# Two of the stores of a matmul-scale-add kernel are issued after a count of ScalarE's copies

## The chip, the cores and the metric

One core of one Trainium2 chip runs the whole program. The metric is the device time of one execution in microseconds (us); the median of three runs stands for a kernel. A profile is of one execution, with times counted from its first instruction.

## The reference

```python
def setup_inputs():
    batch, m, k, n = 16, 512, 1024, 768
    return {
        "x": np.random.randn(batch, m, k).astype(np.float32),
        "weight": np.random.randn(k, n).astype(np.float32),
        "scale": np.float32(0.1),
        "add_value": np.random.randn(batch, m, n).astype(np.float32),
    }

def reference(x, weight, scale, add_value):
    return (scale * np.matmul(x, weight) + add_value).astype(np.float32)
```

With the batch folded into the rows this is one product of 8192 x 1024 by 1024 x 768, scaled, plus a tensor of the result's size. In float32 x is 33.6 MB, add_value and the result are 25.2 MB each, and the weight is 3.1 MB: 87 MB in all.

## The kernel before

**Tiles.** The 8192 rows are 64 tiles of 128 rows. Each partition holds 16 consecutive rows of each block of 2048 (`R = 16`), so a transfer of 8 tiles is one long contiguous run for each partition. SBUF holds 16 tiles of x in float32 (`xs`, 16 slots) and 32 slots of `ao`, in which the tile's add_value lands, the result is made in place, and from which it is stored. The weight first lands in `ao` and is cast to bf16 into `w_bf`.

**The engines.** Every engine has its own hand-written stream, and they meet only at semaphores.

- SyncE issues every transfer in the order of the list `STREAM` (line 22): `w`, `x`, `a` are loads of weight, x and add_value, `o` is a store; the two numbers are the first tile and the count. `sync_engine` (line 87) walks the list. Before an issue it waits for what the transfer needs, through `need(sem, value)`, which emits a wait only if no earlier one on that semaphore was as high. All transfers go through one queue, in that order. The first load of x (line 225) and the last store (line 237) stand outside the list.
- ScalarE and GpSimd (`mover`, line 134) copy x from `xs` into `va`, cast to bf16. A move is four tiles; each of the two engines makes 8 copies for it, and each copy adds 1 to `by_act` or `by_pool`. There are 16 moves and so 128 copies on each engine. A move waits for its x to land (`x_sem`) and for a buffer of `va` to be free (`turned`).
- VectorE (`vector_engine`, line 150) transposes a half move (two tiles) at a time into `xt` (line 162), and finishes two tiles at a time: `ao = mm * scale + ao` from PSUM (line 171), which adds 2 to `made`.
- TensorE (line 205) multiplies: 8 weight loads and 16 matmuls a tile, in PSUM buffers for four tiles.

**Waits on SyncE.** A load of x waits until both copying engines have passed the move that was in its slots (lines 104 and 105). An add_value load waits for the one before it, and from tile 32 on for the landing of the store that frees its slots (lines 109 to 115). A store waits for the store two before it (line 125) and for its own tiles to be made (line 126). Around the change the order of issues is

```python
("x", 32, 8), ("o", 0, 8), ("o", 8, 8), ("a", 32, 8), ("x", 40, 8),
("a", 40, 8), ("x", 48, 8), ("o", 16, 8), ("o", 24, 8), ("a", 48, 4), ("x", 56, 4),
```

Of the kernel before, what the change touches and what calls it, by code (L numbers as in the profile page):

```python
# [27 lines left out]
]  # L28
FIRST, LAST = (0, 8), (56, 8)


@with_exitstack
def kernel(
# [26 lines left out]
    def rows(view, s, n):  # L60
        assert s // R == (s + n - 1) // R
        return view[:, s // R, s % R:s % R + n, :]
# [15 lines left out]
    by_act, by_pool, pool_go, turned, casts, done, made = (  # L78
        tc.alloc_semaphore(name)
        for name in ("by_act", "by_pool", "pool_go", "turned", "casts", "done", "made"))  # L80
# [3 lines left out]
    def slot(t):  # L84
        return (t + G) % A_SLOTS

    def sync_engine(eng):
        loads, stores, known = [], [], {}

        def need(sem, value):  # L90
            if known.get(sem, 0) < value:
                eng.wait_ge(sem, value)
                known[sem] = value

        for op, s, n in STREAM:
            last = s + n - 1
            if op == "w":
                dst = ao[:, s:s + n, :].rearrange("p (c r) n -> p c (r n)", r=2)
                move, sem = eng.dma_start(dst, w_v[:, s // 2:(s + n) // 2, :]), w_sem[s // 4]
            elif op == "x":  # L100
                k = s % X_SLOTS
                if last >= X_SLOTS:
                    moved = 8 * (last + 1 - X_SLOTS) // MOVE
                    need(by_act, moved)
                    need(by_pool, moved)
                move = eng.dma_start(xs[:, k:k + n, :], rows(x_v, s, n))
                sem = x_sem[k // MOVE]
            elif op == "a":
                if loads and s % G == 0:
                    need(a_sem, 16 * len(loads))  # L110
                if slot(s) == 0:
                    need(casts, KJ)
                if s >= A_SLOTS:
                    i = next(j for j, (a, b) in enumerate(stores) if a <= s - A_SLOTS < a + b)
                    need(o_sem[i % 2], 16 * (i // 2 + 1))
                move = eng.dma_start(ao[:, slot(s):slot(s) + n, :], rows(add_v, s, n))
                if s % G:
                    sem = a_late
                else:
                    sem = a_sem  # L120
                    loads.append((s, n))
            else:
                i = len(stores)
                if i > 1:
                    need(o_sem[i % 2], 16 * (i // 2))
                need(made, MADE + last + 1)
                move = eng.dma_start(rows(out_v, s, n), ao[:, slot(s):slot(s) + n, :])
                sem = o_sem[i % 2]
                stores.append((s, n))
            move.then_inc(sem, 16)  # L130
            if op == "x" and n == 2 * MOVE:
                eng.sem_inc(x_sem[k // MOVE + 1], 16)
# [90 lines left out]
    s, n = FIRST  # L223
# [4 lines left out]
    with tc.tile_critical(no_gpsimd_drain=True):  # L228
        sync_engine(nc.sync)
        mover(nc.scalar, nc.scalar.copy, 0, by_act)  # L230
        nc.scalar.addr_align(HALF_BLOCK, offset=PAST)
        mover(nc.gpsimd, nc.gpsimd.tensor_copy, 1, by_pool, pool_go)
        nc.gpsimd.addr_align(HALF_BLOCK, offset=PAST)
        vector_engine(nc.vector)
        tensor_engine(nc.tensor)
    s, n = LAST
# [36 lines left out]
```

## Time and profile before

| | us |
|---|---|
| median of 3 runs (209.06 to 209.6) | 209.28 |
| span of the profiled execution | 207.5 |
| TensorE busy | 168.4 |
| VectorE busy | 97.8 |
| ScalarE busy | 134.7 |
| GpSimd busy | 135.4 |

The span runs from the first to the last instruction of the program; the time of a run also holds what lies around it, which the profile of this execution doesn't give by itself. In the profile an engine's name with a q (SPq) is its sequencer, which issues transfers. "DMA" in a slice is the mean busy share of the core's 16 DMA engines. The time to landing of a transfer counts from its issue until all 16 engines have reported, so it holds the time in the queue. Line numbers are those of the kernel before.

### The profile page before, as it was taken

What the parts mean: (1) busy time and instruction counts of PE and PEld (TensorE: products, weight loads), DVE (VectorE), ACT (ScalarE), POOL (GpSimd) and SP (SyncE); (2) the same over time, 40 slices, a digit from 0 to 9 for tenths busy, and PEclk for the clock granted to TensorE, in tenths of its full rate; (3) what the DMA queues carried; (4) which work ended last, traced back from release to release, by engine and by line L of the source; (5) the groups of instructions that cost most, each with busy time, mean ns of one, the idle gap of its engine ahead of it and who ended that gap; (6) DMA issues with size and microseconds to landing.
All of it is one profiled execution on the core that took longest, in us unless ns stands there. A gap on an engine that the chain in (4) does not pass through costs nothing.

```text
span 207.5 us, 2310 instructions
## 1 busy us (share of the span) xinstructions
PE 168.4 (81%) x1024; PEld 50.3 (24%) x512; DVE 97.8 (47%) x66; ACT 134.7 (65%) x129; POOL 135.4 (65%) x132
## 2 busy tenths in 40 slices
PE   0000099999999999999999999999999999999400
PEld 0000023333332222222233333333333333333100
DVE  0005525537555555555555554755555555553300
ACT  2059970799999796969696079999970999300000
POOL 0049994799999996969696079999990899400000
PEclk9999999999999999999999999999999999999955
DMA  7999999999999999999999999999999999999993
GB/s 291 417 381 469 403 466 404 455 455 404 404 467 442 411 398 486 393 441 407 445 436 423 423 436 455 411 445 412 441 414 422 437 445 455 460 417 388 412 441 171
DMA packets 4147, 87.06 MB, mean 420 GB/s; under 512 B 432, under 2 KB 432, under 8 KB 944
## 3 DMA queue, kind: packets, MB, share of 16 engines
q1 hardware_dynamic: 4144, 87.03, 98.1%
q14 instruction: 3, 0.02, 0.0%
HBM read 61.87 MB, written 25.17 MB: 419 GB/s over the span
## 4 chain that ended last, share of the span: by engine, by line
PE 81%; DMA 6%; ACT 5%; DVE 1%; issue 1%; DVEq 0%; ACTq 0%
PE mm L197 81%; DMA xs<-in_x_dram 6%; ACT va L147 5%; DVE ao L171 1%; DVE xt L162 1%; ACTq L140 0%; DVEq L160 0%; DVEq L168 0%
## 5 line engine op out<-in xcount | busy, mean ns | idle before, releaser
L197 PE MATMUL mm<-w_bf,xt 128*128 128x512 bf16 (+1 forms) x1024 | 168.4, 328 | 26.0 <-DVE xt L162 26.0
L147 POOL CAST va<-xs 32x1024 bf16<-32x1024 f32 x128 | 135.2, 1056 | 43.1 <-DMA xs<-in_x_dram 24.7
L147 ACT CAST va<-xs 32x1024 bf16<-32x1024 f32 x128 | 133.4, 1042 | 42.1 <-DMA xs<-in_x_dram 25.8
L171 DVE SCALAR_TENSOR_TENSOR ao<-mm,ao 128x1536 f32 (+1 forms) x32 | 56.3, 1758 | 76.5 <-PE mm L197 76.5
L195 PEld LDWEIGHTS <-xt 128*128 128x128 bf16 x512 | 50.3, 98 | 143.6 <-issue 117.6
L162 DVE STREAM_TRANSPOSE xt<-va 128x1024 f32<-128x1024 f32 x32 | 39.4, 1234 | 3.8 <-ACT va L147 2.1
L155 DVE CAST w_bf<-ao 128x3072 bf16<-128x3072 f32 x2 | 4.5, 2240 | 18.1 <-DMA ao<-in_weight_dram 18.1
L136 ACT ACT_TABLE_LOAD x1 | 1.3, 1283 | 1.3 <-SPq L228 1.3
L254 POOL MEMSET const-float32-0.0<- 128x1 f32 x1 | 0.1, 98 | 0.2 <-issue 0.2
L254 POOL MEMSET const-bfloat16-1.0<- 128x1 bf16 x1 | 0.1, 100 | 0.0
L254 POOL MEMSET const-float32-1.0<- 128x1 f32 x1 | 0.1, 98 | 0.0
L254 POOL MEMSET const-uint8-127<- 128x1 uint8 x1 | 0.1, 97 | 0.0
## 6 DMA issues: line engine op xcount, KB each, us to landing
xs<-in_x_dram SPq DMA_DIRECT2D x7, 4096.0 KB, 20.9
ao<-in_add_value_dram SPq DMA_DIRECT2D x7, 3072.0 KB, 17.0
out_dram<-ao SPq DMA_DIRECT2D x6, 3072.0 KB, 27.0
out_dram<-ao SPq DMA_DIRECT2D x1, 6144.0 KB, 35.4
xs<-in_x_dram SPq DMA_DIRECT2D x2, 2048.0 KB, 19.1
ao<-in_weight_dram SPq DMA_DIRECT2D x2, 1536.0 KB, 16.8
ao<-in_add_value_dram SPq DMA_DIRECT2D x2, 1536.0 KB, 14.9
```

Of the source, the lines that this page charges most:

```text
L136: eng.preload_act_table(mybir.ActivationFunctionType.Copy)
L147: copy(va[q % VA_BUFS][32 * b:32 * b + 32, :, a, :], src[32 * a:32 * a + 32, :, b, :]).then_inc(count, 1)
L155: eng.tensor_copy(w_bf[:, s:s + n, :], ao[:, s:s + n, :]).then_inc(casts, n)
L162: eng.transpose(xt[:, 2 * half:2 * half + 2, :, :].rearrange("p i c m -> p (i c m)"), va[move % VA_BUFS][:, q:q + 2 * KC, :, :].bitcast(fp ...
L171: eng.scalar_tensor_tensor(a, mm[:, q:q + 2, 0:N], float(scale), a, op0=mybir.AluOpType.mult, op1=mybir.AluOpType.add).then_inc(made, 2)
L195: eng.ldweights(x_j, tile_position=(0, 0))
L197: m = eng.add_instruction(mybir.InstMatmult(start_tensor_calc=(j == 0), stop_tensor_calc=(j == KJ - 1), tile_size=(P, P), tile_position=(0 ...
L254: nc = _bacc.Bacc("TRN2", target_bir_lowering=False, num_devices=1)
```

## The change

Before the store that starts with tile 0, SyncE also waits until ScalarE has made 58 of its copies, and before the store that starts with tile 16 until it has made 93. No other line is touched.

```diff
 FIRST, LAST = (0, 8), (56, 8)
+HOLD = {0: 58, 16: 93}
...
                 if i > 1:
                     need(o_sem[i % 2], 16 * (i // 2))
                 need(made, MADE + last + 1)
+                if s in HOLD:
+                    need(by_act, HOLD[s])
                 move = eng.dma_start(rows(out_v, s, n), ao[:, slot(s):slot(s) + n, :])
                 sem = o_sem[i % 2]
                 stores.append((s, n))
```

## The prediction

> **What bounds the kernel now.** I read the page first, then the chain of waits, then the sync engine's queue in order of time, then single transfers.
>
> The page's busy times, the slices of PE, clock and DMA, the queue's share, and the start of the chain by line:
>
> ```profile
> PE 168.4 (81%) x1024; PEld 50.3 (24%) x512; DVE 97.8 (47%) x66; ACT 134.7 (65%) x129; POOL 135.4 (65%) x132
> ...
> PE   0000099999999999999999999999999999999400
> ...
> PEclk9999999999999999999999999999999999999955
> DMA  7999999999999999999999999999999999999993
> ...
> q1 hardware_dynamic: 4144, 87.03, 98.1%
> ...
> PE mm L197 81%; DMA xs<-in_x_dram 6%; ACT va L147 5%; DVE ao L171 1%; DVE xt L162 1%; ACTq L140 0%; DVEq L160 0%; DVEq L168 0%
> ```
>
> Two resources are full. TensorE has one unbroken stretch at full granted clock, and the 16 DMA engines are busy for 98.1% of the span. The chain names TensorE, because after its last matmul there is only one finish and one store:
>
> ```profile
> 26.01 168.37 PE mm L197 x1024
> ...
> 194.48 1.76 DVE ao L171
> ```
>
> The last finish ends at 196.24 us. What comes after it is read from the sync engine's queue (start, us, what it issued):
>
> ```profile
> 72.62 0.33 SPq L106 DMA_DIRECT2D xs<-in_x_dram  x1
> 73.05 0.85 SPq L127 DMA_DIRECT2D out_dram<-ao  x2
> 96.01 0.34 SPq L116 DMA_DIRECT2D ao<-in_add_value_dram  x1
> 96.44 0.82 SPq L106 DMA_DIRECT2D xs<-in_x_dram  x1
> ...
> 112.76 0.33 SPq L106 DMA_DIRECT2D xs<-in_x_dram  x1
> 113.20 0.84 SPq L127 DMA_DIRECT2D out_dram<-ao  x2
> 144.95 0.34 SPq L116 DMA_DIRECT2D ao<-in_add_value_dram  x1
> ...
> 196.53 0.33 SPq L237 DMA_DIRECT2D out_dram<-ao  x1
> ```
>
> Asked for one issue at a time, the trace gives the us from issue to landing. In this order: x of tiles 32 to 39 (issued 72.62), the store of 0 to 7 (73.05), x of 48 to 55 (112.76), the store of 16 to 23 (113.20), the store of 48 to 55 (175.5, out of the page's L127 group, whose last start is in the second row here), and the final store (196.53):
>
> ```profile
> xs<-in_x_dram SPq DMA_DIRECT2D x1, 4096.0 KB, 16.0
> out_dram<-ao SPq DMA_DIRECT2D x1, 3072.0 KB, 22.9
> xs<-in_x_dram SPq DMA_DIRECT2D x1, 4096.0 KB, 24.6
> out_dram<-ao SPq DMA_DIRECT2D x1, 3072.0 KB, 31.7
> L127 SPq DMA_DIRECT2D out_dram<-ao x6: 344/398/426, 73.1 to 175.5; - x6
> out_dram<-ao SPq DMA_DIRECT2D x1, 3072.0 KB, 23.8
> out_dram<-ao SPq DMA_DIRECT2D x1, 3072.0 KB, 10.1
> ```
>
> So x of 32 to 39 lands at 72.62 + 16.0 = 88.6, and the store behind it at 73.05 + 22.9 = 95.95, that is 7.35 us later; x of 48 to 55 at 137.4, and the store behind it at 113.20 + 31.7 = 144.9, 7.5 us later. The store of 48 to 55 lands at 199.3 and the final one at 196.53 + 10.1 = 206.6, again 7.3 us later. Each transfer lands one transfer's length behind the one issued before it: the queue works as a line, first in, first out, and a store issued early only stands in it longer. The final store was issued 2.8 us before the one ahead of it had landed. So at the end the line of transfers, not TensorE, sets the time, with 2.8 us of backlog on its slowest engine: **whatever makes the DMA engines run dry anywhere adds itself to the end, and what leaves them full adds nothing.**
>
> **The change part by part.** It adds two waits on the sync engine and moves four store issues; no instruction of another engine, no byte and no order of transfers changes. When are the waits met? ScalarE's copies, from the row at 83.11 (copies 57 to 64, since seven moves of 8 copies come before it) and from 120.41 (copies 81 to 112, the eleventh move and on):
>
> ```profile
> 83.11 8.51 ACT L147 CAST va<-xs 32x1024 bf16<-32x1024 f32 x8 [1.94 <-DVE xt L162]
> ...
> 120.41 34.12 ACT L147 CAST va<-xs 32x1024 bf16<-32x1024 f32 x32 [8.04 <-DMA xs<-in_x_dram]
> ```
>
> Copy 58 is the second of its eight: 83.11 + 2 x 8.51/8 = 85.24. Copy 93 is the thirteenth of its 32: 120.41 + 13 x 34.12/32 = 134.27. From a landing to the issue that waits for it the sync engine takes about 0.07 us (the store lands at 95.95, the add_value issue starts at 96.01), so the stores are issued at about **85.3** instead of 73.05, 12.3 us later, and at about **134.3** instead of 113.20, 21.1 us later.
>
> What is ahead of them in the line? The first store still has x of 32 to 39 ahead, until 88.6: a lead of 3.3 us. The second has x of 48 to 55 ahead, until 137.4: a lead of 3.0 us. Is that lead enough for a store to be ready when its turn comes? The trace has one store with so short a lead, the final one: lead 2.8 us, and it landed 7.3 us after its predecessor, no later than the store of 0 to 7, which had waited 15.6 us in the line (7.35). Both new leads are longer than the one that cost nothing on the slowest engine. The other engines finished the predecessor sooner; what they lost shows in stretches of 2 us (last columns: clock, DMA share, GB/s):
>
> ```profile
> 196.00:198.00 2.00, 0.00 (x0) 0.00 (x0) 0.23 (x1) 0.00 (x0) 0.00 (x0) 0.73 0.89 381
> 198.00:200.00 2.00, 0.00 (x0) 0.00 (x0) 0.00 (x0) 0.00 (x0) 0.00 (x0) 0.50 0.93 393
> ...
> 26.00:194.40 168.40, 168.36 (x1024) 50.30 (x512) 90.30 (x62) 120.64 (x116) 122.81 (x119) 1.00 1.00 431
> ```
>
> Against a share of 1.00 in the body they lack 2 x 0.11 + 2 x 0.07 = 0.36 us on average. That is the upper bound for one hold by the nearest row, 0.7 us for both. A far bound is the kernel's first load, which met an empty line: 12.1 us to land, where x of 32 to 39 took the line from 78.7 to 88.6, 9.9 us (the add_value load ahead of it, issued at 61.68, landed after 17.0), so an empty line costs 2.2 us in all.
>
> ```profile
> DMA to landing us min/median/max: 12.1/12.1/12.1
> 61.68 0.33 SPq L116 DMA_DIRECT2D ao<-in_add_value_dram  x1
> ao<-in_add_value_dram SPq DMA_DIRECT2D x1, 3072.0 KB, 17.0
> ```
>
> Even that whole 2.2 us is shorter than either lead. I take 0 for both holds, with 0.7 kept for the range.
>
> What is queued behind the waits? Behind the first: the store of 8 to 15, the add_value load of 32 to 39, then x of 40 to 47. That add_value load waits for the first store's landing (96.01 follows 95.95), and x of 40 to 47 stands right behind it (96.44). Behind the second: the store of 24 to 31 and the add_value load at 144.95, which follows the store's landing at 144.9. So the issues behind the holds hang on landings, and if the stores land at the same time, nothing behind them moves, and TensorE sees nothing. If the cover were gone, x of 40 to 47 would be late first: ScalarE waited 8.04 us for it before 120.41, and the transposition of its first two tiles leaves little room:
>
> ```profile
> 129.37 1.25 DVE L162 STREAM_TRANSPOSE xt<-va 128x1024 f32<-128x1024 f32 x1 [0.70 <-POOL va L147]
> ```
>
> It ends at 130.62; TensorE needs it after 40 tiles, 26.01 + 40 x 168.37/64 = 131.24, a slack of 0.6 us. A gap above 0.6 us at the first hold would stop TensorE by the rest; but the line of transfers passes the whole gap to the end anyway, so the price stays the gap.
>
> Can the holds gain? The loads ahead of the stores: x of 32 to 39 already takes 9.9 us for 4096 KB, which is 424 GB/s against the body's 431, so there is no more than 0.2 us in it, and TensorE never waits. At the end the engines are uneven: of the last 4 us (40 slices of 0.1 us, packets by their start) one packet starts alone some 0.9 us after all others.
>
> ```profile
> DMA  0099995550000000050000000000000000000000
> GB/s 0 0 737 1475 492 492 246 246 246 0 0 0 0 0 0 0 0 246 0 0 0 0 0 0 0 0 0 0 0 0 0 0 0 0 0 0 0 0 0 0
> ```
>
> Were that engine level with the rest, the end would come 0.9 us sooner; that is the lower bound. Nothing in the hold is aimed at one engine, so I take 0.
>
> The Trainium skill speaks against the change, on the side of the first rival below: DMA: Bandwidth & Descriptors, section Rules for kernel authors, says to issue a DMA early so that its fixed setup overlaps, and the section on the anatomy of one DMA puts the fixed cost at about 2.0 us. By that rule two exposed setups would give an estimate of 4.0 us more, 213.3; but the same page puts most of the fixed cost behind the last byte, and the trace agrees in that the final store, with its lead of 2.8 us, landed on time.
>
> Sum: 207.5 (span) + 0 + 0 = 207.5. The median of the runs is 209.28, so 1.8 us lie around the profiled span; 207.5 + 1.8 = **209.3 us**.
>
> **The rivals.**
> *The line runs dry (slower).* Place: the 16 engines at 88 and 137 us. For it: the holds turn leads of 15.6 and 24.2 us into 3.3 and 3.0, and the mean engine did lack 0.36 us at the final store; with 98.1% busy there is nowhere to get it back. Against it: that store still landed in 7.3 us, and both new leads are longer. Price: 0.36 to 0.6 us a hold (above 0.6 the slack of TensorE goes too), 0.7 to 1.2 in all: 210.0 to 210.5. Were each late issue to pay the whole 2.2 us of an empty line, it would be 4.4 us and 213.7; both leads exceed that, so 0.02 of this case's chance goes there. It decides once a store comes with a lead below about 2.8 us, that is, when the counted copy ends 0.2 to 0.5 us later than reckoned.
> *The engines end more even (faster).* If standing stores are what sets one engine behind, issuing them late levels it: up to 0.9 us, 208.4. For it: the lone last packet. Against: the stores run in the same order at the same times.
> *It doesn't do what it says.* If tiles, not copies, were already the later condition, the waits would pass at once. The stores of 0 to 7 and 16 to 23 were issued straight behind the x load ahead of them (72.62 to 73.05, 112.76 to 113.20), so the condition on finished tiles was long met, and the new waits do bind. This would give 209.3 too and cannot be told by the time.
>
> **How the numbers follow.** Chances: forecast (with the last rival) 0.58, dry line 0.26, more even engines 0.16. Of this kernel about 0.3%, 0.6 us, can be told from no change, and the three cases then are same, slower and faster; a dry line at its lower price would just be told. So slower 0.25, same 0.59, faster 0.16. The likeliest alone spans 208.9 to 209.8, about the spread of the runs; the range takes in half of the more even engines and the dry line up to its upper price: 208.6 to 210.5.
>
> **What would show it.** Right: store issues near 85.3 and 134.3; the store of 0 to 7 some 10.6 us from issue to landing, that of 16 to 23 some 10.6; the next add_value issues still at 96.0 and 144.9; one TensorE stretch of 168.4 us; DMA share still 98%. Wrong: add_value issues later than that, a DMA share below 97%, ScalarE's wait before 120.4 longer, or the last store landing away from 206.6 while the middle stays (the engines' evenness). A first or second store issue after 86 or 135 would mean that the copies were misread.

## The result, and the profile after

The changed kernel took 209.84 us (median of 21 runs, 209.13 to 211.12), the kernel before 209.23 (21 runs beside them, 209.06 to 209.6). The ratio is 1.0035, 95% interval 1.0024 to 1.0045: slower by 0.6 us, just beyond the 0.3% that the prediction took as its bound. The spread is the second result: the runs of before lie within 0.3%, those of the changed kernel within 1%.

The profiled execution of the changed kernel took 210.92 us, one of its longer runs, with a span of 209.1. In its page the lines that answer to those of before are these:

```profile
PE 168.9 (81%) x1024; PEld 50.5 (24%) x512; DVE 97.9 (47%) x66; ACT 134.7 (64%) x129; POOL 135.4 (65%) x132
...
PE   0000099999999999999999999999999999999200
...
DMA  8999999999999999999999999999999999999992
...
q1 hardware_dynamic: 4144, 87.03, 97.7%
```

TensorE still has one unbroken stretch, and the DMA engines are still busy nearly all the time. No engine that computes waits for long at a new place. The sync engine's queue (start, us, what it issued) shows both holds at work:

```profile
72.70 0.33 SPq L107 DMA_DIRECT2D xs<-in_x_dram  x1
85.89 0.82 SPq L130 DMA_DIRECT2D out_dram<-ao  x2
95.83 0.34 SPq L117 DMA_DIRECT2D ao<-in_add_value_dram  x1
96.28 1.22 SPq L107 DMA_DIRECT2D xs<-in_x_dram  x1
...
113.34 0.33 SPq L107 DMA_DIRECT2D xs<-in_x_dram  x1
134.59 0.82 SPq L130 DMA_DIRECT2D out_dram<-ao  x2
145.63 0.34 SPq L117 DMA_DIRECT2D ao<-in_add_value_dram  x1
...
156.87 0.33 SPq L117 DMA_DIRECT2D ao<-in_add_value_dram  x1
157.25 19.18 SPq L130 DMA_DIRECT2D out_dram<-ao  x2
197.11 0.33 SPq L240 DMA_DIRECT2D out_dram<-ao  x1
```

The us to landing of single transfers: the store of tiles 0 to 7 (85.89), the load of x of 48 to 55 (113.34), the store of 16 to 23 (134.59), the last add_value load (156.87) and the final store (197.11):

```profile
out_dram<-ao SPq DMA_DIRECT2D x1, 3072.0 KB, 9.9
xs<-in_x_dram SPq DMA_DIRECT2D x1, 4096.0 KB, 24.7
out_dram<-ao SPq DMA_DIRECT2D x1, 3072.0 KB, 11.0
ao<-in_add_value_dram SPq DMA_DIRECT2D x1, 3072.0 KB, 21.9
out_dram<-ao SPq DMA_DIRECT2D x1, 3072.0 KB, 11.1
```

The first held store landed at 95.8, when it had landed before (95.95): issued 12.8 us later and no later done. The second landed at 145.6, 0.7 us behind the 144.9 of before, because the load ahead of it was already 0.6 us late on its slowest engine (138.0 against 137.4). At the end the final store landed at 208.2 instead of 206.6. Its run took 2.7 us more than that landing, as every profiled run here with a time of its own did (2.68 to 2.72). So the last landing is the time, and the 1.6 us have to be found on the way to it.

Only a part of them is on all engines. The packets' starts in slices of 0.14 us from 203.5 us on, to be set against the lone late packet of before:

```profile
DMA  9840409904404004040000040000000000000000
GB/s 1229 351 176 0 176 0 1931 527 0 176 176 0 176 0 0 176 0 176 0 0 0 0 0 176 0 0 0 0 0 0 0 0 0 0 0 0 0 0 0 0
```

Most engines start their last packet near 204.5, then single ones trail out over 2 us. By the landing records of the two traces, the ninth of the 16 engines to land ended its last store at 205.15 before and at 205.72 after; the last one at 206.60 and at 208.23. So 0.6 us of the 1.6 is common to the engines, and 1 us is added by the last one, which fell further behind the others. A second profile, further down, shows which of the two parts comes back.

Where does it fall behind? On a single engine a packet of a given size nearly always takes the same time: 1.21 us for the 32 KB of an x load, 0.91 for the 24 KB of an add_value load or a store. Apart from the first packets of the run, a few near 180 us and some single ones, the exceptions stand together at the few places where the line turns from loads to stores (at 86, 135 and 175 us) or back (at 101 and 150 us), nearly all in the last packets before the turn. Rows of a view that shows it (from, to, us, busy times; in the last columns clock, DMA share, GB/s), the five us around the turn at 175 us, in the kernel before first and then in the changed kernel:

```profile
172.00:177.00 5.00, 5.00 (x33) 1.56 (x16) 2.91 (x2) 4.90 (x5) 4.70 (x6) 1.00 1.03 442
```

```profile
172.00:177.00 5.00, 5.00 (x33) 1.50 (x16) 2.77 (x3) 4.88 (x6) 4.76 (x5) 1.00 1.00 393
```

Packets are counted where they start, so share and GB/s swing together, and only their quotient speaks: 442/1.03 = 429 before, 393/1.00 = 393 after. The engines don't stand idle; they move 8% less while they are busy. The sum over the 16 engines of what packets took beyond their usual time, counting excesses of 0.09 us and more, in us:

```
turn at (us)                       86   101   135   150   175
before                            2.2   0.0   0.4   0.1   0.3
changed kernel                    0.0   5.0   1.0   3.3   7.0
changed kernel, second profile    0.0   5.6   0.1   3.0   7.3
```

So the holds do take something away: the stretched packets at 86 us, ahead of the first held store. More comes back at the later turns. What the turn at 175 us costs can be read at the landings: the last add_value load, whose last packets stand there, landed 7.4 us behind the load ahead of it before (177.06 and 169.66 us), and 8.4 us behind it in the changed kernel (178.72 and 170.34). That is 1.0 of the 1.6 us; the other 0.7 had come before it, and nothing to speak of was won or lost behind it.

### The profile page after: what moved, and what is told of

Same layout as the page of the kernel before. It is cut to its first block, busy times and chain, and to the rows that moved or that the text cites. A ratio compares the mean times of both kernels' runs of the same rounds, so it can differ in the third digit from the quotient of the medians.

```text
span 209.1 us, 2311 instructions
## 1 busy us (share of the span) xinstructions
PE 168.9 (81%) x1024; PEld 50.5 (24%) x512; DVE 97.9 (47%) x66; ACT 134.7 (64%) x129; POOL 135.4 (65%) x132
## 3 DMA queue, kind: packets, MB, share of 16 engines
q1 hardware_dynamic: 4144, 87.03, 97.7%
## 4 chain that ended last, share of the span: by engine, by line
PE 81%; DMA 6%; ACT 5%; DVE 1%; issue 1%; DVEq 0%; ACTq 0%
PE mm L200 81%; DMA xs<-in_x_dram 6%; ACT va L150 5%; DVE ao L174 1%; DVE xt L165 1%; ACTq L143 0%; DVEq L163 0%; DVEq L171 0%
## 6 DMA issues: line engine op xcount, KB each, us to landing
xs<-in_x_dram SPq DMA_DIRECT2D x7, 4096.0 KB, 20.9
```

## The experiments

The theory formed from these two traces: a store issued late unsettles the DMA engines at later turns between loads and stores, and one engine ends far behind. Rivals: the line runs dry at a hold, the added instructions cost something, or every hold has a price of its own. All ratios are to the kernel before, run beside them on the same chip. Diffs are against the changed kernel.

**The waits alone, already met.**

```diff
-HOLD = {0: 58, 16: 93}
+HOLD = {0: 48, 16: 80}
...
-                    need(by_act, HOLD[s])
+                    eng.wait_ge(by_act, HOLD[s])
```

> The two waits are kept as instructions but ask for 48 and 80 copies, which the loads of x just ahead of them have already waited for, so nothing is delayed. Theory (the late issue itself unsettles the 16 DMA engines): as before, ratio 0.999 to 1.001, spread of the runs as narrow as before's (0.3%). Rival (the added instructions cost or shift something on SyncE): a ratio like the changed kernel's, 1.003 or more, with runs spread over 1%.

Measured: 0.9999 (0.9989 to 1.0009), runs from 209.05 to 209.31. The instructions cost nothing that can be told; it is the delay.

**One hold at a time.**

```diff
-HOLD = {0: 58, 16: 93}
+HOLD = {0: 58}
```

> Only the store of tiles 0 to 7 is held (58 copies). Theory (each late issue unsettles the DMA engines at the next switches between loads and stores): some of the loss, ratio 1.001 to 1.003, the last engine falling behind after 95 us. Rival (the line runs dry at the hold at 137 us, where the lead is shortest): nothing, 1.000.

```diff
-HOLD = {0: 58, 16: 93}
+HOLD = {16: 93}
```

> Only the store of tiles 16 to 23 is held (93 copies). Theory (late issues unsettle the engines): some of the loss, 1.001 to 1.003, all of the trace up to 120 us as before's. Rival (line runs dry at 137 us): all of the loss, 1.003 to 1.004, and a DMA share under 0.95 in the 2 us behind 136.

Measured: the first alone 1.0006 (0.9995 to 1.0017), not told from none; the second alone 1.0026 (1.0011 to 1.0042), most of the loss. The stretched packets, as in the table above:

```
turn at (us)            86   101   135   150   175
first hold alone       0.0   3.7  10.4   0.2   0.2
second hold alone      7.0   0.1   0.0   2.2   5.6
```

A held store has no stretched packets ahead of it, as at 86 in the first row and at 135 in the second (and few in the changed kernel, 1.0 at 135). The turn back to loads behind it (101, 150) then has them, and so has the next turn to a store that was not held (135, 175). Behind that turn it is quiet again, as the first row shows. A stretch at 135 us costs the end little, one at 175 us much. With the first hold alone the ninth engine to land stays 0.7 us later than before from 137 us to the end (205.82 against 205.15), but the last one ends only 0.7 us behind it, against 1.45 before; why the last engine loses less there, one profile doesn't show.

The rival asked for a DMA share under 0.95 in the 2 us behind 136, and with the second hold alone it is 0.89. But the kernel before has 0.82 in the 2 us ahead of 136, so that sign decides nothing. In the changed kernel, over both holds, the same view as above has

```profile
84.00:88.00 4.00, 4.00 (x27) 1.17 (x12) 2.10 (x2) 3.90 (x5) 3.82 (x4) 1.00 1.03 444
88.00:92.00 4.00, 4.00 (x27) 1.19 (x13) 1.71 (x2) 3.93 (x4) 3.76 (x5) 1.00 0.93 399
134.00:138.00 4.00, 4.00 (x27) 1.18 (x13) 1.61 (x2) 3.63 (x4) 3.82 (x4) 1.00 0.92 391
138.00:142.00 4.00, 4.00 (x26) 1.18 (x12) 2.91 (x2) 3.82 (x4) 3.76 (x5) 1.00 1.07 461
```

and the kernel before

```profile
84.00:88.00 4.00, 4.00 (x27) 1.19 (x13) 2.68 (x2) 3.90 (x5) 3.76 (x5) 1.00 1.04 432
88.00:92.00 4.00, 4.00 (x26) 1.17 (x12) 1.71 (x2) 3.55 (x4) 3.70 (x4) 1.00 0.96 412
134.00:138.00 4.00, 4.00 (x27) 1.25 (x13) 1.59 (x2) 3.90 (x5) 3.81 (x4) 1.00 0.91 387
138.00:142.00 4.00, 4.00 (x27) 1.17 (x12) 2.34 (x2) 3.90 (x5) 3.77 (x4) 1.00 1.04 449
```

The shares swing by as much in both, since packets are counted where they start. The landings decide: the ninth engine ended each held store 7.3 us behind the load ahead of it, as it did before, in the changed kernel and with either hold alone. That leaves no room for a gap: the line does not run dry at the holds.

**The changed kernel again.**

> The changed kernel once more, for a second profile. If its loss is the engines' unevenness: ratio 1.002 to 1.005, runs spread over 1% again, and the last landing and the DMA shares near 101, 150 and 175 us other than in the first profile. If it is a fixed gap or wait: the same places in both profiles.

Measured: 1.0035 (1.0015 to 1.0055), runs from 209.12 to 211.24; the profiled one took 209.56. The places are those of the first profile (second row of the changed kernel in the table above). What differs between the two is how far behind the last engine ends: 1.1 us behind the ninth here, 2.5 in the first profile. The ninth ended its last store at 205.74, as in the first profile (205.72). So the common 0.6 us comes back and the last engine's extra lag does not: here it is less than the 1.45 us of before, and the last landing is 0.3 us later than before instead of 1.6. At the turn at 175 us the last add_value load again lost 0.8 us (8.2 behind the load ahead, 7.4 before).

**Earlier, and later.** The same two stores, held for less or for more copies:

```diff
-HOLD = {0: 58, 16: 93}
+HOLD = {0: 53, 16: 85}
```

> Both stores held, but only for 53 and 85 copies: issued near 78 and 126 us, some 8 us sooner than in the changed kernel, with 10 and 11 us of lead. Theory (a store that comes late unsettles the engines by how little is left in the line): less of the loss, ratio 1.000 to 1.002. Rival (a hold unsettles them however early): 1.003 again, packets stretched near 101, 150 and 175 us.

```diff
-HOLD = {0: 58, 16: 93}
+HOLD = {0: 55, 16: 89}
```

> Held for 55 and 89 copies: issued near 80.2 and 130.1 us, when the transfer ahead of the load of x has landed (78.7 and 127.6) and the load of x alone is in the line, 7 to 8 us before it lands. If what counts is that no more than one transfer is left in the line: the loss of the changed kernel, 1.002 to 1.005, packets stretched near 101, 150 and 175 us. If what counts is a lead under some 3 to 4 us: none, 0.999 to 1.001.

```diff
-HOLD = {0: 58, 16: 93}
+HOLD = {0: 64, 16: 98}
```

> Held for 64 and 98 copies: issued near 92.2 and 140 us, about 3.5 us and 2.5 us after the loads of x ahead have landed. The line runs dry by about 4.5 and 3.5 us (with 1 us from an issue to the first packet), which nothing can give back: 8 us, ratio 1.035 to 1.042, TensorE standing still behind 131 us. If gaps were hidden by TensorE's lead instead: under 1.02.

Measured: early 1.0004 (0.9995 to 1.0013), in between 1.0002 (0.9994 to 1.0011), late 1.0504 (1.0489 to 1.0518). With 53 and 55 copies the stretched packets are where they are before (at 86 us), with 0.0 us at 175. In the kernel in between the stores were issued at

```profile
80.76 0.82 SPq L130 DMA_DIRECT2D out_dram<-ao  x2
95.97 0.34 SPq L117 DMA_DIRECT2D ao<-in_add_value_dram  x1
96.41 0.86 SPq L107 DMA_DIRECT2D xs<-in_x_dram  x1
...
130.08 0.82 SPq L130 DMA_DIRECT2D out_dram<-ao  x2
```

that is 7.8 and 7.3 us before the load ahead landed (88.56 and 137.35 by the landing records), with nothing but that load in the line. So it is not that one transfer alone is left that counts, but the lead: somewhere between 7 and 3 us it starts to unsettle the engines.

The late kernel shows what a dry line looks like. Its holds end at

```profile
72.65 0.33 SPq L107 DMA_DIRECT2D xs<-in_x_dram  x1
92.89 0.82 SPq L130 DMA_DIRECT2D out_dram<-ao  x2
...
117.67 0.37 SPq L107 DMA_DIRECT2D xs<-in_x_dram  x1
146.30 0.82 SPq L130 DMA_DIRECT2D out_dram<-ao  x2
```

and in this order the two loads and the two stores took to landing

```profile
xs<-in_x_dram SPq DMA_DIRECT2D x1, 4096.0 KB, 15.8
xs<-in_x_dram SPq DMA_DIRECT2D x1, 4096.0 KB, 26.3
out_dram<-ao SPq DMA_DIRECT2D x1, 3072.0 KB, 8.7
out_dram<-ao SPq DMA_DIRECT2D x1, 3072.0 KB, 8.7
```

The first store came 4.4 us after the load had landed (88.45), the second 2.3 us after (143.97), and each took 8.7 us with an empty line ahead of it, 1.4 more than the 7.3 of a store in a full line. That is 5.8 + 3.7 = 9.5 us of the 10.6 by which the median grew. The packets show the same gaps: none was under way from 87.98 to 93.74 us and from 143.45 to 147.14. The expectation had 8: the first store came 0.9 us further behind its load than reckoned, and each start cost 1.4 us and not 1. In the first gap the DMA share is zero, and later TensorE stands still for 4.14 and 1.35 us (start, busy us, and idle us before in brackets):

```profile
88.00:92.00 4.00, 4.00 (x26) 1.24 (x13) 1.71 (x3) 3.90 (x5) 3.78 (x4) 1.00 0.00 0
```

```profile
137.30 43.75 PE L200 MATMUL mm<-w_bf,xt 128*128 128x512 bf16 x256 [4.14 <-DVE xt L165]
182.40 20.98 PE L200 MATMUL mm<-w_bf,xt 128*128 128x512 bf16 x128 [1.35 <-DVE xt L165]
```

**The store behind the holds.** If the price is paid at the next turn to a store that was not held, a hold of that store, too, should take the loss away. The store of tiles 32 to 47 is the next one:

```diff
-HOLD = {0: 58, 16: 93}
+HOLD = {0: 58, 16: 93, 32: 124}
```

> As the changed kernel, and the store of tiles 32 to 47 is held for 124 copies too, issued near 174 us instead of 157, with 3 us of lead. In the profiles the packets before a held store are not stretched, but those before the next store that has stood in the line for long are (175 us in the changed kernel). Theory: that stretch goes, ratio 1.000 to 1.002. Rival (each hold unsettles the engines for the rest): more loss than with two, 1.004 to 1.008.

> All three held (58, 93, 124) once more, beside the changed kernel's 1.0035: 0.999 to 1.001 and again no stretch near 175 us if the first result was no accident; 1.002 or more if it was.

```diff
-HOLD = {0: 58, 16: 93}
+HOLD = {32: 124}
```

> Only the store of tiles 32 to 47 is held for 124 copies. Theory (the loss is paid at a later switch from loads to a store that stood long; behind this hold there is none): as before, 0.999 to 1.001. Rival (each late issue costs by itself): 1.001 to 1.003.

```diff
-HOLD = {0: 58, 16: 93}
+HOLD = {16: 93, 32: 124}
```

> The stores of tiles 16 to 23 and 32 to 47 are held (93 and 124 copies). The second alone gave 1.0026. Theory (its loss is the stretch before the next store that stood long, at 175 us, and a hold of that one takes it away): 0.999 to 1.001 and no stretched packets near 175 us. Rival (a hold has its price wherever): 1.002 to 1.004.

```diff
-HOLD = {0: 58, 16: 93}
+HOLD = {0: 58, 16: 93, 32: 113}
```

> The third hold is met 12 us sooner, at 113 copies (near 162 us, 15 us before the load ahead has landed, with three loads in the line). If it is the late issue of the third store that takes the loss away: the loss is back, 1.002 to 1.005, with the stretch near 175 us. If it is the wait itself or the shift on SyncE: 1.000.

Measured, with the stretched packets:

```
holds                       ratio (95%)                86   101   135   150   175
0, 16, 32 late              1.0001 (0.9992-1.0010)    0.0   8.1   0.0   4.5   0.2
0, 16, 32 late, again       1.0007 (0.9996-1.0019)    0.0   2.4   0.3   6.3   0.4
32 late                     1.0001 (0.9992-1.0010)    3.0   0.1   0.0   0.1   0.2
16, 32 late                 0.9999 (0.9990-1.0007)    5.8   0.1   0.0   1.8   0.4
0, 16 late, 32 early        1.0030 (1.0014-1.0047)    0.0   8.0   0.0   9.6   7.9
```

Adding a third hold takes the loss of two away, and the stretch at 175 us with it; the same third wait met 11 us sooner brings both back. That settles the place of the loss: the second hold leads to stretched packets ahead of the next store that has stood in the line, and at 175 us these reach the last engine's landing. The landings say so in all profiles but the late kernel's, whose line ran dry: without a stretch at 175 us the last add_value load lands 7.3 to 7.4 us behind the load ahead of it (nine profiles), with one 8.2 to 8.5 us (the changed kernel twice, the second hold alone, and the early third hold). From there to the last landing it is 29.0 to 29.6 us in all of them. The sync engine's queue and the five us around the turn, in the kernel with three holds:

```profile
156.26 0.33 SPq L117 DMA_DIRECT2D ao<-in_add_value_dram  x1
174.09 2.91 SPq L130 DMA_DIRECT2D out_dram<-ao  x2
```

```profile
172.00:177.00 5.00, 5.00 (x33) 1.47 (x15) 2.71 (x3) 4.90 (x5) 4.70 (x6) 1.00 1.10 474
```

and in the one whose third hold is early:

```profile
157.00 0.33 SPq L117 DMA_DIRECT2D ao<-in_add_value_dram  x1
163.08 13.42 SPq L130 DMA_DIRECT2D out_dram<-ao  x2
```

```profile
172.00:177.00 5.00, 5.00 (x33) 1.57 (x16) 2.81 (x3) 4.88 (x6) 4.76 (x5) 1.00 1.15 452
```

GB/s by share is 474/1.10 = 431 and 452/1.15 = 393, as 429 before and 393 in the changed kernel. The last add_value load, which the stretched packets belong to, took 20.8 and 21.9 us to land, as 20.9 before and 21.9 in the changed kernel. The first run with three holds has its place in this, too: with its engines level to 0.3 us at the end, it took 209.27, no less than before, because in that execution TensorE ended late (the final store was issued at 197.69). No version here is told from the kernel before on the fast side; that TensorE's end leaves no room for it is shown by this one execution alone.

## Why the prediction was right in part

The measured time, 209.84, lies in the range of 208.6 to 210.5, but the likeliest case, no change, was not what happened: the kernel is slower by 0.35%, for which the prediction had a chance of 0.25, and by a cause that it had not priced on that side.

- *Two full resources, and the line of transfers setting the end.* Right. The time follows the last landing in every profile, and a gap in the line goes to the end nearly whole (9.5 of 10.6 us in the late kernel).
- *When the holds end.* Roughly right: 85.89 and 134.59 instead of 85.3 and 134.3. In this execution the row of copies 57 to 64 began 0.6 us later than in the profile before; in the second profile of the changed kernel the issue was at 85.57.
- *The lead is enough, cost 0 on the line.* Right as to gaps, and now shown from both sides: no gap at leads of 2.6 and 3.4 us; with a dry line, 1.4 us on top of the time waited. The first rival, a dry line, falls. The 0.36 us that the prediction read as the mean engine's loss was no measure of one: the DMA share of short stretches swings that far where no gap is (0.91 to 1.04 in the rows of before above). The estimate of 4.0 us falls too, which the prediction drew from the fixed cost of 2.0 us in the Trainium skill, DMA: Bandwidth & Descriptors, section Anatomy of one DMA. The page gives that figure for transfers that GpSimd issues, and all transfers here are issued by SyncE; a start that is exposed cost 1.4 us here, and at these holds none was. The advice under Rules for kernel authors on that page, to issue a DMA early so that its fixed setup overlaps, points the right way here, but for another reason and with 0.6 us.
- *What leaves the engines full adds nothing.* This is the step that failed. From it the prediction took 0 for any hold that leaves no gap. The engines stayed full, but the issue time of a store, with order and bytes the same, changed how long packets take at the later turns: around 175 us the engines moved 393 GB/s by share instead of 429, and the last add_value load lost 1.0 and 0.8 us there in the two profiles. Every kernel with that stretch is slower than before and none without it can be told from before, so this is where most of the 0.6 us of the median is lost.
- *The engines' evenness.* Not priced on the side of a loss. The prediction wrote "Nothing in the hold is aimed at one engine, so I take 0", and gave the term a bound on the gain side alone, 0.9 us. The last engine ended 1 us further behind the ninth in one profile and 0.3 us less far in the other, so its lag goes both ways; with it the last landing of the same kernel differed by 1.4 us. The row with the lone late packet had shown that a single engine sets the end, so its lag could have been priced both ways.
- *The range.* That it held the time is in part luck: its upper end was reckoned from a dry line, and there was none.
- *The chain behind the holds.* Right for the first: the add_value issue at 95.83 (96.0 forecast). For the second 145.63 instead of 144.9, by the lag of the last engine in the load ahead (138.0 against 137.4), not by a gap at the hold.
- *That the change does what it says.* It does, and with the waits already met the time is that of before.

What stays open is why. In these profiles a store that came with a lead of 2.1 to 3.4 us made the turns behind it costly until the next store that had stood in the line for 16 us or more was passed; what in the DMA engines carries that memory, no run here shows. The hold of tiles 0 to 7 and that of 16 to 23 also delay the store right behind them in the list, and no run holds one of the two without the other. Nor was it tried which lead between 3.4 and 7.3 us is the edge.

## What to carry to other kernels

Where a full transfer queue sets the end, delaying an issue behind a compute count is free only while a comfortable lead remains: here 7 us were free, 3 us cost 0.35% and an empty line cost its whole gap and 1.4 us. Look at what the DMA engines move while they are busy and at the slowest of them, not at their busy share: the share hardly moved (98.1 to 97.7%) while the last landing moved by 1.6 us. And when the runs of a kernel spread more than those of the one before, look for a cause of chance timing before explaining the median.

## What the runs showed of the hardware

- A packet ahead of a turn between loads and stores can take well over its usual time on many engines at once: at 175 us in the changed kernel 14 packets of 24 KB took 0.2 to 1.0 us more than their 0.91 us, and before a single one did, 0.3 us more. Whether it happens depends on how long ago the next store, or the one before, was issued.
- The load of x of tiles 40 to 47 is issued right behind an add_value load. It held the sync engine for 0.62 to 0.90 us in the seven kernels whose first store was not held or held with a long lead (96.41 in the queue of the kernel in between), and for 1.16 to 1.26 us in those whose first store came late (96.28 in that of the changed kernel). The slow issue goes with the stretched packets; which causes which is open.
- After TensorE had stood for 4.14 us in the late kernel, the granted clock fell, and a window of 4 us held 17 matmuls instead of 26; after its stand of 1.35 us the clock stayed at 1.00. The rows around the longer one:

```profile
134.00:138.00 4.00, 0.70 (x4) 0.33 (x3) 2.00 (x2) 3.90 (x5) 3.82 (x4) 0.98 0.91 393
138.00:142.00 4.00, 4.00 (x17) 0.93 (x7) 2.03 (x2) 3.90 (x5) 3.76 (x5) 0.59 1.10 475
142.00:146.00 4.00, 4.00 (x26) 1.17 (x12) 1.38 (x1) 3.93 (x4) 3.76 (x5) 1.00 0.12 49
```
